# Weaving the start of each layer into the down projection of the layer before it, in a four-layer decoder trunk on eight cores

## The chip, the cores and the metric

The kernel runs on all 8 cores of one Trainium2 chip, cores 0 to 3 on one die and 4 to 7 on the other. Each core has two sequences of its own and works through them without the other cores. The time is device time of the slowest core, in microseconds (us). In slow runs the cores of a die, or of both, show a granted TensorE clock of 0.81 instead of 1.00 for part of the run, and the execution takes longer. Fast runs are compared with fast runs below, and single stages where the clock is 1.00. PE is TensorE's matmuls, PEld its weight loads, DVE VectorE, ACT ScalarE, POOL GpSimd.

## The reference

```python
# B=16, SEQ=2048 (+16 meta tokens), D_MODEL=1024, D_FF=2816, DEPTH=4, windows (2, 4, 8, 16)
for i in range(DEPTH):
    u = rms_norm(h, norm_g[i, 0])
    if i % 2 == 0: m = pool_mixer(u, ...)        # causal window means per channel group, minus u, then 256x256 matmuls
    else:          m = short_conv_mixer(u, ...)  # w_in (1024x3072), gated 3-tap conv, w_out (1024x1024)
    h = h + rms_norm(m, norm_g[i, 1])
    u = rms_norm(h, norm_g[i, 2])
    f = conv_ffn(u, ...)                         # up (1024x5632), 3-tap conv, silu(gate)*val, down (2816x1024)
    h = h + rms_norm(f, norm_g[i, 3])
```

So every sub-layer has a norm ahead of it and one behind it, and the norm ahead of a layer needs the finished h of the layer before.

## The kernel before

A core cuts its 2 x 2064 tokens into four *groups* of 1032, and a group into three *tiles* (0, 1, 2) of 344. It takes one group through all four layers, then the next. Channels lie on the partitions, so a tile of h is eight blocks of 128 x 344.

The kernel is written as a list of operations with what each reads and writes. A small list scheduler then fixes each engine's order at build time: it looks at the next few operations of an engine (the window) and takes the first whose inputs are ready by its own estimates.

```python
SCHED_WINDOW = {"pe": 12, "act": 8, "dve": 8, "pool": 10, "sp": 6}
...
finish[k] = st + o.cost + (0.25 if e == "pe" else 0.15)
```

A norm ahead of a sub-layer squares a tile whole (one ScalarE instruction), sums over the channels with eight matmuls against a matrix of ones, and gets 1/rms from Ln and Exp on ScalarE. The norm behind a sub-layer works chunk by chunk as results arrive:

```python
def norm_stats(t):
    P.op("act", I("activation", out=sq[:, :, 0:N], in_=h[:, :, o:o + N], func=AF.Square), ...)
    sbank, skey = bank("S")
    P.op("pe", [I("matmul", ps[sbank][:, 0:N], lhsT=ones[:], rhs=sq[:, c, 0:N], ...) for c in range(KC)], ...)
    return rstd_from_ss(sbank, skey, N)
...
class PostNorm:
    def chunk(self, m, pbank, pkey):     # copy to a scratch vector, square into sq[m], one ones-matmul
        ...
    def finish(self):                    # after 8 chunks: 1/rms, then per block
        # VectorE: fr = fr * g * r      GpSimd: h = h + fr
```

The down projection, called D below, is 8 chunks of 22 matmuls per tile:

```python
def ffn_d_tile(l, t):
    pn = PostNorm(l, 3, t)
    for m in range(KC):
        fb, fk = bank("C6")                        # 6 PSUM banks in turn
        P.op("pe", [... for j in range(JC)], ...)  # 22 matmuls
        pn.chunk(m, fb, fk)
    pn.finish()
```

The first projection of a convolution layer goes over four weight slots and, in each, over the tiles. With two PSUM banks per role it works in this order and no other:

```python
def sconv_s1(l):
    for sg in range(4):
        for t in range(NT):
            for mm in range(2):
                ca, va, ba = bank("A"), bank("B"), bank("C")   # shortened
                # 3 x 8 matmuls, then a few ACT and DVE steps on the PSUM results
```

A pooling layer has four stages per tile: a (norm statistics), b (window sums on VectorE), c (group matmuls and their post-norm), and the norm ahead of the feed-forward part. The main loop runs the layers one after another (cut):

```python
for li, l in enumerate(layers):
    if l % 2 == 0:
        ffn_prefetch(l)
        pool_phase(l, half)           # a, b, c, ffn_pre as a pipeline over the tiles
    else:
        for t in range(NT): sconv_pre_tile(l, t, half)
        sconv_s1(l); ffn_prefetch(l)
        for t in range(NT): sconv_s2_tile(l, t)
        for t in range(NT): ffn_pre_tile(l, t, half)
    ffn_u(l)
    ...
    for t in range(NT): ffn_d_tile(l, t)
```

## Time and profile before

The first three executions took 6521.72, 6352.34 and 6243.06 us. The profiled one was slow (6566.94 us), so stages are read where the clock is 1.00.

| Stage, core 0, clock 1.00 | us |
|---|---|
| D, three tiles | 80.4 |
| gap from D to a convolution layer's first matmul | 19.2 to 19.5 |
| its first projection, 576 matmuls | 87.9 |
| these three together ("convolution boundary") | 187.5 |
| gap from D to the up projection of a pooling layer | 86.2 to 87.6 |
| that up projection | 182.8 to 184.4 |
| D, gap and up projection ("pooling boundary") | 351 |

A group has two convolution boundaries (layers 0 to 1, 2 to 3) and one pooling boundary (1 to 2): 8 and 4 in the whole run. The rows of the stretches behind this table are shown in the prediction.

### The profile page before, as it was taken

To read this page: it belongs to the slowest core of one execution; us is meant where nothing else is said; L and a number is where in the kernel's file an instruction comes from. 1 tells how busy PE (TensorE), PEld (TensorE's weight loads), DVE (VectorE), ACT (ScalarE), POOL (GpSimd) and SP (SyncE) were. 2 spreads that over 40 slices of the span, in tenths; PEclk is the share of its full clock that TensorE was granted. 3 is DMA by queue.
4 is the path that set the end of the run, shared out by engine and by line. 5 is a ranking of instruction groups with operands and counts; after the bars stand their busy time and mean duration, and the time that the engine had idled before them with its cause. 6 is when DMAs were issued, how large, how long until landed. Compare 5 with 4: busy or idle time off the path is not lost.

```text
span 6565.4 us, 101733 instructions; the slowest of 8 cores (6455.2 to 6565.4 us)
## 1 busy us (share of the span) xinstructions
PE 5628.6 (86%) x33984; PEld 3499.4 (53%) x33984; DVE 3616.6 (55%) x6114; ACT 2391.1 (36%) x4689; POOL 1109.8 (17%) x1212
## 2 busy tenths in 40 slices
PE   3998869897798959989499886999949999789999
PEld 2655536564455636556265553655626556446555
DVE  5646474663746566464655647446356355463562
ACT  3334333433334333343433433324243233332333
POOL 2012121201212030121101212111120120211111
PEclk6999979897899979999699996877867778778777
DMA  5536243542535335353352524335144253152351
GB/s 89 70 44 84 33 65 43 72 68 71 74 46 75 52 49 69 44 84 53 74 72 43 84 32 65 43 48 76 22 94 59 33 74 52 20 74 33 52 84 30
DMA packets 433069, 385.67 MB, mean 59 GB/s; under 512 B 41072, under 2 KB 371056, under 8 KB 432560
## 3 DMA queue, kind: packets, MB, share of 16 engines
q0 software_dynamic: 422784, 345.01, 37.9%
q1 hardware_dynamic: 9776, 34.15, 1.5%
q8 instruction: 285, 4.67, 0.3%
q14 instruction: 224, 1.84, 0.1%
HBM read 707.20 MB, written 16.91 MB: 110 GB/s over the span
## 4 chain that ended last, share of the span: by engine, by line
PE 78%; DVE 10%; issue 7%; ACT 2%; DMA 2%; POOL 1%; DVEq 0%; ACTq 0%; POOLq 0%; SPq 0%
PE ps L41 78%; DVE vbuf L41 4%; DVE ugrp L41 3%; DVE actbuf L41 2%; DMA stg<-hin 1%; ACT vbuf L41 1%; POOL h L41 1%; DMA out<-stg 1%; ACT sq L41 1%; ACT stg L41 0%; DVE halom L41 0%; ACT L41 0%; DVEq L235 0%; ACTq L235 0%; ACT h L41 0%
## 5 line engine op out<-in xcount | busy, mean ns | idle before, releaser
L41 PE MATMUL ps<-ugrp,ring 128*128 128x346 bf16 (+1 forms) x21504 | 3484.4, 327 | 187.3 <-DVE ugrp L41 136.1
L41 PEld LDWEIGHTS ps<-ugrp,ring 128*128 128x128 bf16 x21504 | 2162.9, 102 | 1505.6 <-issue 306.5
L41 DVE SCALAR_TENSOR_TENSOR vbuf<-vbuf,par 128x344 f32<-128x344 f32 x1152 | 946.9, 864 | 1560.2 <-ACT vbuf L41 1542.4
L41 PE MATMUL ps<-actbuf,wa 128*128 128x344 bf16 x9984 | 1647.4, 325 | 0.0
L41 DVE SCALAR_TENSOR_TENSOR vbuf<-ps,par,vbuf 128x344 f32<-128x344 f32 x2112 | 1216.1, 576 | 255.5 <-ACT vbuf L41 147.1
L41 PEld LDWEIGHTS ps<-actbuf,wa 128*128 128x128 bf16 x9984 | 1017.7, 102 | 552.8
L41 ACT ACTIVATE vbuf<-vbuf 128x344 f32<-128x344 f32 x1248 | 610.3, 489 | 1503.3 <-DVE vbuf L41 1498.0
L41 POOL TENSOR_TENSOR h<-h,vbuf 128x344 f32<-128x344 f32 x768 | 729.0, 949 | 2160.8 <-DVE vbuf L41 1789.6
L41 DVE TENSOR_TENSOR actbuf<-vbuf,ps 128x344 bf16<-128x344 f32 x1248 | 640.3, 513 | 731.4 <-ACT vbuf L41 676.2
L41 ACT ACTIVATE vbuf<-ps 128x344 f32<-128x344 f32 (+1 forms) x768 | 351.0, 458 | 1450.5 <-PE ps L41 1443.9
L41 ACT ACTIVATE vbuf<-ps,par 128x344 f32<-128x344 f32 x1248 | 680.6, 545 | 468.1 <-PE ps L41 352.3
L41 PE MATMUL ps<-sq,ones 128*128 128x344 bf16 x1536 | 461.0, 397 | 349.4 <-ACT sq L41 347.4
L41 POOL DMA_DIRECT2D ring<-ffn_w_up x256 | 225.3, 881 | 2514.2 <-PE ps L41 2483.5
L41 PEld LDWEIGHTS ps<-sq,ones 128*128 128x128 bf16 x1536 | 177.5, 119 | 524.3 <-issue 407.0
L41 DVE SCALAR_TENSOR_TENSOR ugrp<-h,par,vbuf 128x344 bf16<-128x344 f32 x576 | 368.4, 646 | 78.5 <-ACT vbuf L41 43.4
L41 PE MATMUL ps<-ugrp,pwres 128*128 128x344 bf16 x384 | 113.7, 461 | 290.0 <-DVE ugrp L41 236.8
L41 ACT ACTIVATE sq<-h 128x2752 bf16<-128x2752 f32 x96 | 239.1, 2490 | 90.3 <-POOL h L41 90.3
L41 ACT ACTIVATE sq<-ps 128x344 bf16<-128x344 f32 x576 | 261.6, 454 | 18.5 <-PE ps L41 18.5
L41 PEld LDWEIGHTS ps<-ugrp,pwres 128*128 128x128 bf16 x384 | 51.5, 139 | 344.1 <-issue 301.3
L41 ACT ACTIVATE vbuf<-ps,epsb 128x344 f32<-128x344 f32 x192 | 104.9, 547 | 329.0 <-PE ps L41 314.7
L41 DVE SCALAR_TENSOR_TENSOR actbuf<-h,par,vbuf 128x344 f32<-128x344 f32 x192 | 114.1, 616 | 195.6 <-ACT vbuf L41 194.2
L41 DVE TENSOR_TENSOR actbuf<-actbuf 128x688 f32<-128x688 f32 (+3 forms) x240 | 211.1, 881 | 3.6
(31 smaller groups left out, 959.3 us busy)
## 6 DMA issues: line engine op xcount, KB each, us to landing
ring<-ffn_w_up POOLq DMA_DIRECT2D x224, 768.0 KB, 11.2
wa<-ffn_w_down POOLq DMA_DIRECT2D x32, 1536.0 KB, 19.1
ring<-sc_w_in POOLq DMA_DIRECT2D x96, 512.0 KB, 10.4
wa<-ffn_w_down POOLq DMA_DIRECT2D x32, 1280.0 KB, 32.9
stg<-hin SPq DMA_DIRECT2D x32, 512.0 KB, 4.5
out<-stg SPq DMA_DIRECT2D x32, 512.0 KB, 2.7
wa<-sc_w_out POOLq DMA_DIRECT2D x8, 1536.0 KB, 13.6
ring<-ffn_w_up POOLq DMA_DIRECT2D x32, 256.0 KB, 5.2
```

The costliest lines, as they stand in the source:

```text
L41: return lambda e: getattr(e, name)(*args, **kw)
```

## The change

Its intent is to fill these gaps. The operations of D for tiles 1 and 2 are written alternately, chunk by chunk, with the start of the next layer for tiles 0 and 1. The start of a convolution layer is its norm; that of a pooling layer is its norm and window sums. What belongs to tile 2 follows D. Three things go with it: a smaller scheduling window for TensorE and a latency dropped from the scheduler's estimates, weights of a pooling layer's up projection requested earlier, and fixed shares of scratch vectors and norm banks for the two interleaved streams.

```diff
+MERGE_D = True
-SCHED_WINDOW = {"pe": 12, "act": 8, "dve": 8, "pool": 10, "sp": 6}
+SCHED_WINDOW = {"pe": 8, "act": 8, "dve": 8, "pool": 10, "sp": 6}
...
+                        if e == "pe" and ops[d].eng == "pe":
+                            f -= 0.25
...
         def vec():
+            vp = ctx["vpool"]
+            if vp == "main":   # 14 of 16 scratch vectors   (cut)
+            elif vp == "bg":   # the other 2                (cut)
...
+        def merged(main_gen, bg_gen, per=1):
+            while True:
+                ctx.update(sbank=6, vpool="main")
+                ...  next(main_gen)          # one chunk of D
+                ctx.update(sbank=7, vpool="bg")
+                ...  next(bg_gen)            # one piece of the next layer's start
...
+                    if nxt is None or not MERGE_D:
+                        for t in range(NT):
+                            ffn_d_tile(l, t)
+                    else:
+                        bgf = bg_pool_gen if nxt % 2 == 0 else sconv_pre_gen
+                        ffn_d_tile(l, 0)
+                        for t in range(1, NT):
+                            merged(ffn_d_gen(l, t), bgf(nxt, t - 1, half))
+                        ctx.update(vpool="bg")
+                        gl = bgf(nxt, NT - 1, half)
+                        if nxt % 2 == 0:
+                            ctx.update(vpool=None)
+                            pool_stage_c(nxt, 0, half)
+                            ctx.update(vpool="bg")
+                        run(gl)
+                        ctx.update(vpool=None)
```

(Cut: functions turned into generators, a buffer of its own for the pooling's edge fix, the earlier `ffn_prefetch(nxt)`, and the skipping of work that has been done early.)

More of the change, by code (lines that the diff above doesn't have):

```diff
@@ L286, in build @@
         ones = sb("ones", [128, 128], BF16)
+        cfix = sb("cfix", [128, 16], F32)
         stg = [sb(f"stg{i}", [128, D], F32) for i in range(2)]
@@ L314, in region_to @@
                 reg_mode[t] = mode
-        cnts = {"psA": 0, "psB": 0, "psC": 0, "psC6": 0, "psS": 0, "vec": 0, "ring": 0, "stg": 0, "alt": 0}
+        cnts = {"psA": 0, "psB": 0, "psC": 0, "psC6": 0, "psS": 0, "vec": 0, "ring": 0, "stg": 0, "alt": 0, "vecm": 0, "vecb": 0}
         def g_ap(l, i, c):
@@ L340, in build @@
         P.op("dve", I("memset", epsb[:], EPS), writes=["eps"])
+        ctx = {"sbank": None, "vpool": None}
         def bank(role):
             if role in ("S", "T"):
+                if role == "S" and ctx["sbank"] is not None:
+                    i = ctx["sbank"]
+                    return i, f"ps{i}"
                 i = 6 + (cnts["psS"] % 2)
@@ L357, in vec @@
         def vec():
-            i = cnts["vec"] % NVEC
-            cnts["vec"] += 1
+            vp = ctx["vpool"]
+            if vp == "main":
+                i = cnts["vecm"] % (NVEC - 2)
+                cnts["vecm"] += 1
+            elif vp == "bg":
+                i = NVEC - 2 + (cnts["vecb"] % 2)
+                cnts["vecb"] += 1
+            else:
+                i = cnts["vec"] % NVEC
+                cnts["vec"] += 1
             return vecs[i], f"vec{i}"
@@ L447, in norm_stats, with prenorm_ugrp_gen @@
             return rstd_from_ss(sbank, skey, N)
-        def prenorm_ugrp(l, i, t):
+        def prenorm_ugrp_gen(l, i, t):
             o = t * N
             r, kr = norm_stats(t)
+            yield
             for c in range(KC):
@@ L455, in prenorm_ugrp, with run @@
                      reads=[hk(t), kr, "par"], writes=[f"ug{t}"], cost=0.5)
+                if c % 3 == 2:
+                    yield
+        def run(gen):
+            for _ in gen:
+                pass
+        def prenorm_ugrp(l, i, t):
+            run(prenorm_ugrp_gen(l, i, t))
         class PostNorm:
@@ L466, in chunk @@
             def chunk(self, m, pbank, pkey):
+                sq_to("chunks")
                 sc = self.scale_fn(m) if self.scale_fn is not None else 1.0
@@ L557, in ffn_pre_tile, with sconv_pre_gen, sconv_pre_tile @@
                 ugrp_halo_save(halo_f[l], f"halof{l}")
-        def sconv_pre_tile(l, t, half):
+        def sconv_pre_gen(l, t, half):
             if t == 0:
                 ugrp_halo_fill(halo_m[l], f"halom{l}", half)
-            prenorm_ugrp(l, 0, t)
+            yield from prenorm_ugrp_gen(l, 0, t)
             if t == NT - 1:
                 ugrp_halo_save(halo_m[l], f"halom{l}")
+        def sconv_pre_tile(l, t, half):
+            run(sconv_pre_gen(l, t, half))
         def ukeys_of(t):
@@ L616, in ffn_u, with ffn_d_gen @@
                     slots.append(load_wup_slot(l, sg + 2))
-        def ffn_d_tile(l, t):
+        def ffn_d_gen(l, t):
             pn = PostNorm(l, 3, t)
@@ L625, in ffn_d_tile @@
                 pn.chunk(m, fb, fk)
+                yield
             pn.finish()
+            yield
+        def ffn_d_tile(l, t):
+            run(ffn_d_gen(l, t))
+        def merged(main_gen, bg_gen, per=1):
+            alive = True
+            while True:
+                ctx.update(sbank=6, vpool="main")
+                try:
+                    next(main_gen)
+                except StopIteration:
+                    break
+                if alive:
+                    ctx.update(sbank=7, vpool="bg")
+                    for _ in range(per):
+                        try:
+                            next(bg_gen)
+                        except StopIteration:
+                            alive = False
+                            break
+            ctx.update(sbank=7, vpool="bg")
+            run(bg_gen)
+            ctx.update(sbank=None, vpool=None)
         def sconv_s1(l):
@@ L685, in pool_stage_a, with pool_stage_b_gen @@
             pool_r[t] = norm_stats(t)
-        def pool_stage_b(l, t, half):
+        def pool_stage_b_gen(l, t, half):
             o = t * N
@@ L707, in pool_stage_b @@
                      reads=[pukey], writes=[hkey], cost=0.1)
+                yield
                 cur, lo, curkey = pu, 0, pukey
@@ L719, in pool_stage_b @@
                     cur, lo, curkey = dstb, nlo, dkey_
+                yield
                 sfin = cur[:, :, HP - lo:HP - lo + N]
@@ L726, in pool_stage_b, with bg_pool_gen @@
                     for cc in range(2):
-                        tmpv, kt = vec()
-                        P.op("dve", I("tensor_tensor", out=tmpv[:, 0:16], in0=sfin[:, cc, 0:16], in1=cnt[:, g, :], op=ALU.mult),
-                             reads=[curkey, "cnt"], writes=[kt], cost=0.1)
-                        P.op("dve", I("tensor_tensor", out=ugrp[:, 2 * g + cc, HC + o:HC + o + 16], in0=tmpv[:, 0:16],
+                        P.op("dve", I("tensor_tensor", out=cfix[:, 0:16], in0=sfin[:, cc, 0:16], in1=cnt[:, g, :], op=ALU.mult),
+                             reads=[curkey, "cnt"], writes=["cfix"], cost=0.1)
+                        P.op("dve", I("tensor_tensor", out=ugrp[:, 2 * g + cc, HC + o:HC + o + 16], in0=cfix[:, 0:16],
                                       in1=pu[:, cc, HP:HP + 16], op=ALU.subtract),
-                             reads=[kt, pukey], writes=[f"ug{t}"], cost=0.1)
+                             reads=["cfix", pukey], writes=[f"ug{t}"], cost=0.1)
+        def pool_stage_b(l, t, half):
+            run(pool_stage_b_gen(l, t, half))
+        def bg_pool_gen(l, t, half):
+            pool_stage_a(l, t, half)
+            yield
+            yield from pool_stage_b_gen(l, t, half)
         def pool_stage_c(l, t, half):
@@ L745, in pool_stage_c, with pool_phase @@
             pn.finish()
-        def pool_phase(l, half):
-            stages = (pool_stage_a, pool_stage_b, pool_stage_c, ffn_pre_tile)
+        def pool_phase(l, half, skip_ab=False):
+            stages = (pool_stage_c, ffn_pre_tile) if skip_ab else (pool_stage_a, pool_stage_b, pool_stage_c, ffn_pre_tile)
             for step in range(NT + len(stages) - 1):
@@ L751, in pool_phase @@
                     t = step - k
+                    if skip_ab and st is pool_stage_c and t == 0:
+                        continue
                     if 0 <= t < NT:
@@ L807, in build @@
                 for li, l in enumerate(layers):
+                    merged_pre = MERGE_D and li > 0
                     if l % 2 == 0:
-                        ffn_prefetch(l)
-                        pool_phase(l, half)
-                    else:
-                        for t in range(NT):
-                            sconv_pre_tile(l, t, half)
+                        if l not in pre_wup:
+                            ffn_prefetch(l)
+                        pool_phase(l, half, skip_ab=merged_pre)
+                    else:
+                        if not merged_pre:
+                            for t in range(NT):
+                                sconv_pre_tile(l, t, half)
                         sconv_s1(l)
@@ L820, in build @@
                     ffn_u(l)
-                    if li + 1 < len(layers) and layers[li + 1] % 2 == 1:
-                        sconv_prefetch(layers[li + 1])
-                    for t in range(NT):
-                        ffn_d_tile(l, t)
+                    nxt = layers[li + 1] if li + 1 < len(layers) else None
+                    if nxt is not None:
+                        if nxt % 2 == 1:
+                            sconv_prefetch(nxt)
+                        else:
+                            ffn_prefetch(nxt)
+                    if nxt is None or not MERGE_D:
+                        for t in range(NT):
+                            ffn_d_tile(l, t)
+                    else:
+                        bgf = bg_pool_gen if nxt % 2 == 0 else sconv_pre_gen
[10 more added lines that the diff above has]
+                        ctx.update(vpool=None)
                 for tb in range(NBLK):
```

## The prediction

> **What bounds the kernel now.** I read four views of the profile before, in this order: spans and clocks of the cores, the page, a table of stretches of core 0 at the two kinds of layer boundary, and who waited for whom.
>
> The cores first, because the three timed runs spread from 6243 to 6522 us.
>
> ```profile
> core 0: 6565.4 us, clock 0.847
> core 4: 6455.2 us, clock 0.866
> ```
>
> The profiled run was a slow one. Cut into 100 us pieces, each core shows dense stretches at a granted clock of 1.00 for part of the run and of 0.81 for the rest (cores 0 and 1 change at about 4000 us, 4 and 5 back at about 1900 us). The unit of work repeats: four groups of tokens, each four layers. At clock 1.00 one group of core 0 lasts 1552 us (the down projection of the last layer ends at 1549.5 and at 3101.5). So a run at full clock would be 1549.5 + 3 x 1552 + 21 for the last store = 6227 us, an estimate, close to the fastest run's 6243. What is above that in the other runs is the slow clock. I therefore work at full clock and add the clock at the end.
>
> Then the page:
>
> ```profile
> PE 5628.6 (86%) x33984; PEld 3499.4 (53%) x33984; DVE 3616.6 (55%) x6114; ACT 2391.1 (36%) x4689; POOL 1109.8 (17%) x1212
> ...
> PE 78%; DVE 10%; issue 7%; ACT 2%; DMA 2%; POOL 1%; DVEq 0%; ACTq 0%; POOLq 0%; SPq 0%
> ```
>
> TensorE is the bound, but 14% of it is idle, and a tenth of the chain that ended last is VectorE. The stretches say where. Columns: length, busy time of PE, PEld, DVE, ACT, POOL, then granted clock, DMA share, GB/s.
>
> ```profile
> 313.20:393.60 80.40, 80.40 (x553) 53.81 (x550) 17.33 (x20) 22.86 (x54) 17.06 (x19) 1.00 0.27 33
> 393.60:412.90 19.30, 5.42 (x20) 2.27 (x19) 13.80 (x19) 10.96 (x11) 8.92 (x10) 0.61 0.71 109
> 417.40:501.20 83.80, 83.80 (x571) 55.44 (x570) 52.78 (x101) 24.65 (x48) 7.69 (x9) 0.99 0.45 58
> 714.40:794.80 80.40, 80.40 (x553) 53.82 (x550) 17.32 (x20) 22.88 (x54) 17.90 (x20) 1.00 0.15 19
> 794.80:882.40 87.60, 27.75 (x104) 12.74 (x102) 80.64 (x139) 38.72 (x68) 29.12 (x28) 0.61 0.18 26
> 882.40:909.60 27.20, 10.74 (x51) 5.73 (x51) 14.93 (x20) 8.64 (x10) 7.13 (x8) 0.63 1.07 163
> 909.60:1066.80 157.20, 155.66 (x1026) 97.11 (x1027) 105.94 (x200) 60.67 (x129) 13.32 (x16) 0.98 0.47 64
> ```
>
> Rows 1 and 4 are the down projection ("D") of a layer: TensorE full, VectorE 22% busy. Row 2 is the boundary before a convolution layer: 19.3 us from the last D matmul to the first of the next layer. Rows 5 and 6 are the boundary before a pooling layer: TensorE waits while VectorE is busy 80.6 of 87.6 us, and the up projection is dense only from 909.6, 114.8 us after D ended. The same gaps recur in all groups of core 0: 19.2 to 19.5 us eight times and, up to the first up-projection matmul, 86 to 88 us four times; they keep their length at clock 0.81. The waits of TensorE agree:
>
> ```profile
> PE ps L41 <- DVE ugrp L41: 372.9, 44, 15.9
> PE ps L41 <- ACT sq L41: 347.4, 152, 11.6
> ```
>
> It waits for the normalised or pooled input (written by VectorE) and for the squares of a norm (ScalarE): exactly the stages that the change moves.
>
> **What the Trainium skill says.** (1) Perfetto Trace Analysis, Optimization Strategy: where the most-contended engine changes over time, interleaving the regimes may help. That fits rows 4 and 5. (2) TensorE: Matmul & The Clock Gate, Part 2, step 1: matmuls stay in program order, only weight loads are pulled ahead. So a norm's sum matmul put into D stalls D if its squares are late; the trace shows such a stall as "<-ACT sq". (3) The same page, Part 1: dense matmuls on three cores of a die bring the clock of the whole die to 13/16. The 0.81 agrees; "the whole die" does not (cores 0 and 1 still run at 1.00 while 2 and 3 run at 0.81 before 2700 us). (4) GPSIMD Engine Reference, section 1, Specifications: GpSimd shares SBUF interfaces with VectorE and contends when a VectorE instruction has two SBUF inputs. The trace agrees with it: the scale step of a post-norm, two SBUF inputs, beside GpSimd's adds into h, has a mean of 864 ns, the one with a PSUM input 576 ns.
>
> **The change, part by part.** D of tile 0 stays. D of tiles 1 and 2 gets, between its eight chunks, the start of the next layer for tiles 0 and 1; that of tile 2 follows D. There are three such boundaries in a group: two to convolution layers, one to a pooling layer, so 8 and 4 in all. No arithmetic is added or removed; sums of the norms get a fixed PSUM bank each (6 for D, 7 for the early work) and the 16 scratch vectors are split 14 and 2.
>
> *Convolution boundary.* What is moved for one tile is a square of 2.5 us, eight ones-matmuls (1.2 us at full clock), two short activations (1.1 us) and eight VectorE steps (646 ns each, 5.2 us). D of one tile is 26.8 us (80.4 / 3) with 7.6 us of post-norm on VectorE, so this fits. The next layer starts on tile 0 at once when D ends. One weight slot on tiles 0 and 1 is 2 x 6 x 8 matmuls at 146 ns = 14.0 us. Tile 2 is ready later: evict and sum 1.5, rsqrt 1, eight post-norm steps 7.6 (one timeline entry), last add 1.2, square 2.5, ones 1.2, rsqrt 1.1, eight norm steps 5 to 7 between the layer's own VectorE work: 21 to 23 us after D. Weights for the next slot can't be used earlier, because the two PSUM banks of each role are taken in program order. So a stall of about 7 us is left, plus 2.4 us of ones-matmuls now inside D. Gain 19.3 - 7 - 2.4 = about 10 us, times 8 = 80 us.
>
> *Pooling boundary.* The pooling of one tile costs VectorE, from the groups by shape: (114.1 scale + 211.1 adds + 83.6 final + 36.1 halo copies) / 24 tiles = 18.5 us. With the post-norm 7.6 that is 26.1 us in a D of 26.8: VectorE is nearly full there, and h of a tile is final only about 12 us into the next D, its rsqrt 17 us into it. So pooling of tile 0 runs from 17 to beyond the end of D of tile 1, tile 1's starts about 21 us into D of tile 2, and some 13 of its 18.5 us are left when D ends. After D VectorE has 13 + 7.6 (post-norm of tile 2) + 7.6 (post-norm of the pooled tile 0) + 18.5 (pooling of tile 2) = 46.7 us before tile 2's group matmuls can start. Before, these start at 873.9, 79.1 us after D. That is 32 us sooner. After it come one more post-norm of tile 1 that was earlier hidden (+7), and less waiting later, since VectorE idles 9.6 us before 891.8 in the kernel before (about -10). Net about 35, less 2.4 for the ones-matmuls in D: 33 us, times 4 = 132 us.
>
> *The rest.* The scheduler's TensorE window goes from 12 to 8 and its 0.25 us latency between TensorE operations is dropped. While tile 2's pooled matmuls are not ready, 16 operations (8 + 8 ones) stand ahead of the up projection, more than either window, so this order stays: 0 us, give or take 20. The earlier weight prefetch gives nothing, since no dense stretch waits for the ring's DMA.
>
> Sum: 80 + 132 = 212 us. Full clock: 6227 - 212 = 6015 us, ratio 0.966.
>
> **The rivals.**
> - *D stalls.* There is one buffer of squares, used whole by an early norm and in chunks by D's own sums. From chunk 1 on, D's squares wait until the early norm's eight ones-matmuls are done, some 17 to 20 us into D. D survives because six PSUM banks hold its chunks (6 x 3.35 = 20 us). If the squares are 5 us later (VectorE busy with pooling), each merged D stalls by that: 5 x 8 tiles before pooling layers and less in the 16 before convolution layers, 40 to 80 us back. For it: row 5's VectorE load. Against: banks and my times just fit. Time then about 6080.
> - *VectorE becomes the bound of the pooling boundary.* It is in my sum; if GpSimd's adds stretch pooling from 18.5 to 22 us, everything runs over by another 4 us per tile: 10 us x 4 = 40 us back.
> - *The clock takes it back.* Denser TensorE work could keep more cores at 0.81. A wholly slow group costs about 220 us more (the last one takes 6541.2 - 4769.4 = 1772 us from D's end to D's end, against 1552). For: 0.81 is seen only in dense phases. Against: the cores change state in the long gaps, and full-clock runs have dense phases of 280 us. Then 6150 to 6300 in a slow run, with nothing wrong in the schedule.
> - *A better tail.* Were the up projection let in before tile 2's pooled matmuls, 15 us more per pooling boundary: 5950.
>
> **Range and chances.** Runs before have a median 125 us above full clock. After, I take 6015 + about 105 = 6120 us. The low end, 5980, is full clock with a slightly better tail; the high end, 6290, is a run as slow as the middle ones before plus a stalling D. Faster by over 2% needs 125 us of the 212; both boundaries would have to give half of what I expect for it to fail. Faster 0.82, within 2% 0.15, slower 0.03.
>
> **What would show it.** Right: the boundary before convolution layers shrinks from 19.3 us to near zero with a stall of 5 to 9 us some 14 us later; the table of stretches shows VectorE over 80% busy in D of tiles 1 and 2 before a pooling layer; the gap from D to the first up-projection matmul is 50 to 60 us instead of 87; a three-tile D stays within 80.4 + 3 us at clock 1.00. Wrong: D longer than 86 us, with waits for squares inside it (rival 1); a pooling gap over 70 us (rival 2); same gaps gained but the dense stretches at 0.81 for longer (rival 3).

## The result, and the profile after

On the same chip, 13 executions of each:

| | fast runs, us | median of all | range of all |
|---|---|---|---|
| before | 6240.64 to 6249.09 (seven), 6291.63 | 6249.09 | 6240.64 to 7018.77 |
| after | 6117.10 to 6120.38 (six) | 6236.01 | 6117.10 to 6877.29 |

The ratio of fast runs is 0.9791, with a 95% interval of 0.9766 to 0.9815. Ratios here are the mean time of one kernel's fast runs over that of the other's in the same rounds, so they are not quite the ratio of the medians that are quoted. The change is faster, by about 2%. Whether by more than 2% is unclear: the interval lies on both sides of that line, and without the one run of 6291.63 us, which counts as fast, the ratio of means is 6118.6 / 6243.3 = 0.980. In fast runs it gained about 123 us, where 212 had been worked out for full clock.

The profiled execution after was a slow one. First its clocks by die, then lines of the page for all engines and for the chain that ended last, then three of TensorE's waits on core 0 (total us, count, mean):

```profile
die 0 (median of its cores): 6206.5 us, clock 0.899
die 1 (median of its cores): 6224.5 us, clock 0.897
```

```profile
PE 5390.3 (86%) x33984; PEld 3387.8 (54%) x33984; DVE 3604.8 (58%) x6114; ACT 2375.5 (38%) x4689; POOL 1113.2 (18%) x1212
...
PE 76%; DVE 10%; issue 7%; ACT 3%; POOL 2%; DMA 2%; DVEq 0%; ACTq 0%; POOLq 0%; SPq 0%
```

```profile
PE ps L42 <- ACT sq L42: 295.3, 146, 11.6
...
PE ps L42 <- DVE ugrp L42: 259.7, 33, 16.5
...
PE ps L42 <- DVE vbuf L42: 78.3, 32, 6.2
```

The counts of instructions are the same as before. TensorE's share of the span is still 86%: busy time and span shrank together, because less of this run was at 0.81, so this share says nothing about the change. The waits do: those for the normalised or pooled input (`ugrp`) fell from 372.9 to 259.7 us and those for squares from 347.4 to 295.3. But the wait for `vbuf` has doubled, from 37.4 us in 16 waits to 78.3 in 32. Here TensorE waits for VectorE to read a PSUM bank (a product into a scratch vector) before it may overwrite it.

**The convolution boundary.** Stretches of core 0 before: the gap, then the first 10.8 us of the projection. Columns as in the prediction.

```profile
2698.30:2717.70 19.40, 5.39 (x19) 2.26 (x19) 13.92 (x19) 10.96 (x11) 8.99 (x10) 0.59 0.69 108
2717.70:2728.50 10.80, 10.80 (x59) 6.55 (x60) 7.78 (x16) 2.20 (x5) 0.00 (x0) 0.79 0.01 2
```

The same boundary after: D, the projection's first matmuls, a hole, and the rest in two parts.

```profile
2665.70:2747.90 82.20, 82.20 (x564) 54.88 (x563) 27.08 (x37) 29.68 (x60) 16.93 (x19) 1.00 0.25 31
2748.50:2758.20 9.70, 9.68 (x67) 6.20 (x64) 6.84 (x8) 2.75 (x6) 6.62 (x8) 1.00 0.71 111
2758.20:2769.00 10.80, 2.41 (x9) 1.11 (x10) 2.51 (x5) 4.00 (x4) 2.09 (x3) 0.75 0.50 94
2769.00:2785.20 16.20, 16.20 (x95) 9.85 (x96) 13.43 (x29) 4.31 (x8) 2.67 (x3) 0.85 0.13 16
2785.20:2846.30 61.10, 61.10 (x420) 40.50 (x418) 37.07 (x69) 17.76 (x34) 4.75 (x6) 1.00 0.54 74
```

The gap behind D is 0.6 us now (2747.9 to 2748.5), and then TensorE works for 9.7 us and is nearly idle for 10.8: 2.41 us busy, with 9 matmuls. The projection takes 97.9 to 102.4 us (100.4 on average) instead of 87.9, and D takes 82.2 instead of 80.4. Together 183.3 instead of 187.5: of the 19.3 us, 4.2 are gained. The timeline of TensorE, VectorE and ScalarE says what the hole is (start, length; in brackets the engine's idle time ahead and who ended it):

```profile
2749.81 8.37 PE L42 MATMUL ps<-ugrp,ring 128*128 128x346 bf16 x56
...
2751.36 7.57 DVE L42 SCALAR_TENSOR_TENSOR vbuf<-vbuf,par 128x344 f32<-128x344 f32 x8 [3.18 <-ACT vbuf L42]
...
2760.79 2.50 ACT L42 ACTIVATE sq<-h 128x2752 bf16<-128x2752 f32 x1 [1.62 <-POOL h L42]
...
2763.43 2.36 PE L42 MATMUL ps<-sq,ones 128*128 128x344 bf16 x8 [5.25 <-ACT sq L42]
...
2767.12 1.26 DVE L42 SCALAR_TENSOR_TENSOR ugrp<-h,par,vbuf 128x344 bf16<-128x344 f32 x2 [8.19 <-ACT vbuf L42]
...
2768.30 0.51 DVE L42 TENSOR_TENSOR vbuf<-vbuf,ps 128x346 f32<-128x346 f32 x1
...
2768.95 16.28 PE L42 MATMUL ps<-ugrp,ring 128*128 128x346 bf16 x94 [3.16 <-DVE vbuf L42]
```

This is tile 2's chain, link by link: its post-norm on VectorE, the adds on GpSimd, the square, the ones-matmuls, 1/rms, the norm steps. Its first link filled the gap before as well: there VectorE did tile 2's post-norm (7.57 us, as now) ahead of tile 0's norm, for which the first matmul waited. The first 64 matmuls, on tiles 0 and 1, cover 9.4 us of the chain (the 56 shown take 8.37). Then two more things hold TensorE. It reaches the ones-matmuls of tile 2 in its fixed order and waits 5.25 us for the square. And the projection's first VectorE step (2768.30, product of a PSUM result and a scratch vector) stands in VectorE's order behind tile 2's first two norm steps, so that the two banks of the role come free only then: 3.16 us more, "<-DVE vbuf".

**The pooling boundary**, core 0 after: D of tiles 0, 1 and 2, the time up to tile 2's group matmuls, from there to the dense up projection, and that.

```profile
2330.80:2357.50 26.70, 26.70 (x185) 17.92 (x184) 2.10 (x4) 7.00 (x17) 1.45 (x2) 1.00 0.65 90
2357.50:2386.00 28.50, 28.50 (x197) 19.01 (x196) 14.29 (x22) 12.78 (x24) 7.25 (x8) 1.00 0.01 1
2386.00:2414.20 28.20, 27.06 (x186) 17.98 (x185) 22.39 (x35) 9.77 (x19) 8.01 (x8) 1.00 0.00 1
2414.20:2474.60 60.40, 18.56 (x71) 7.41 (x68) 52.51 (x74) 25.01 (x46) 23.28 (x22) 0.59 0.00 1
2474.60:2510.00 35.40, 16.71 (x72) 8.71 (x73) 23.49 (x33) 15.83 (x27) 13.03 (x15) 0.64 0.91 141
2510.00:2665.80 155.80, 154.98 (x1026) 96.52 (x1027) 104.69 (x198) 60.76 (x129) 13.38 (x16) 0.99 0.46 65
```

VectorE was busy 17.3 us in the 80.4 us of D before; now it is 2.10 + 14.29 + 22.39 = 38.8 us. That is the moved work. But in the fourth row it still has 52.51 us to do, in 60.40, and TensorE's 18.56 us lie beside it. The gap from D to the first up-projection matmul is 64.7 us on average over three such boundaries (62.0 to 68.9) instead of 87, D is 85.2 instead of 80.4, and the total is 332.8 (328.6 to 335.0) instead of 351: a gain of 18 us (over all cores, in the boundaries without the clock of 0.81: 351.0 and 333.0). The fifth row is as long as before: there it was 35.7 us (873.9 to 909.6), here it is 35.4.

Three waits inside these rows, from the timeline of the same core:

```profile
2410.74 0.31 PE L42 MATMUL ps<-sq,ones 128*128 128x344 bf16 x1 [1.14 <-ACT sq L42]
...
2430.82 0.99 ACT L42 ACTIVATE vbuf<-ps,par 128x344 f32<-128x344 f32 x2 [11.01 <-DVE vbuf L42]
...
2491.28 7.57 DVE L42 SCALAR_TENSOR_TENSOR vbuf<-vbuf,par 128x344 f32<-128x344 f32 x8 [8.28 <-ACT vbuf L42]
```

The first is D itself waiting for squares. In the second the eviction of tile 0's group matmuls waits 11 us for a scratch vector that VectorE has yet to read, and VectorE is then idle for 6.67 us. That makes this boundary an exception: from D's end to tile 2's group matmuls it takes 60.4 us, and 50.5 to 52.5 at the other three of this core, where VectorE is busy 97% of the time. The third is in the fifth row: VectorE, the bound of the row above, is idle for 8.28 us, because here it waits on the chain of one tile.

### The profile page after: what moved, and what is told of

It reads as the page before. It is cut to its first block, busy times and chain, and to the rows that moved or that the text cites. A ratio compares the mean times of both kernels' runs of the same rounds, so it can differ in the third digit from the quotient of the medians.

```text
span 6234.5 us, 101591 instructions; the slowest of 8 cores (6191.8 to 6234.5 us)
## 1 busy us (share of the span) xinstructions
PE 5390.3 (86%) x33984; PEld 3387.8 (54%) x33984; DVE 3604.8 (58%) x6114; ACT 2375.5 (38%) x4689; POOL 1113.2 (18%) x1212
## 4 chain that ended last, share of the span: by engine, by line
PE 76%; DVE 10%; issue 7%; ACT 3%; POOL 2%; DMA 2%; DVEq 0%; ACTq 0%; POOLq 0%; SPq 0%
PE ps L42 76%; DVE vbuf L42 4%; DVE ugrp L42 3%; DVE actbuf L42 2%; POOL h L42 2%; ACT vbuf L42 2%; DMA stg<-hin 1%; ACT sq L42 1%; DMA out<-stg 1%; ACT stg L42 0%; DVE halom L42 0%; DVEq L238 0%; ACT L42 0%; ACTq L238 0%; POOLq L238 0%
## 5 line engine op out<-in xcount | busy, mean ns | idle before, releaser
L42 PE MATMUL ps<-ugrp,ring 128*128 128x346 bf16 (+1 forms) x21504 | 3352.4, 318 | 190.5 <-DVE ugrp L42 84.1
L42 PEld LDWEIGHTS ps<-ugrp,ring 128*128 128x128 bf16 x21504 | 2093.0, 99 | 1447.0 <-issue 352.3
L42 PE MATMUL ps<-actbuf,wa 128*128 128x344 bf16 x9984 | 1555.8, 314 | 0.0
L42 PEld LDWEIGHTS ps<-actbuf,wa 128*128 128x128 bf16 x9984 | 990.9, 99 | 504.6
L42 PE MATMUL ps<-sq,ones 128*128 128x344 bf16 x1536 | 411.7, 373 | 293.4 <-ACT sq L42 290.9
L42 ACT ACTIVATE sq<-h 128x2752 bf16<-128x2752 f32 x96 | 239.2, 2492 | 101.9 <-POOL h L42 101.9
```

The source lines that it names most:

```text
L42: return lambda e: getattr(e, name)(*args, **kw)
```

## The experiments

Twelve kernels ran. Each diff is against the kernel after unless it says otherwise. "Undisturbed die" is a die that stayed at full clock in an execution whose other die did not.

**1 to 3: which part gives what.** The merge for convolution layers alone, for pooling layers alone, and for none (all the rest of the change kept). In these rounds no run of the kernel before was at full clock (the lowest, 6342.16 us, had all cores at 0.89 to 0.90), so there are no ratios.

```diff
# convolution only
-merged_pre = MERGE_D and li > 0
+merged_pre = MERGE_D and li > 0 and l % 2 == 1
-if nxt is None or not MERGE_D:
+if nxt is None or not MERGE_D or nxt % 2 == 0:
# pooling only: the same with the parities swapped
# nothing merged:
-MERGE_D = True
+MERGE_D = False
```

> Only the 8 boundaries before convolution layers are merged into the down projection; those before pooling layers run as in the kernel before. From the two traces (187.5 us from start of the down projection to the end of the first convolution projection before, 183.3 after) the theory expects 4.2 us x 8 = 34 us under the kernel before, so about 6209 us in a fast run; up to 19 us less if the scheduler's new window and latency give the unexplained rest. My prediction's size (10 us each) would give 6163.

> Only the 4 boundaries before pooling layers are merged. From the traces (351 us from start of the down projection to the end of the up projection before, 333 after): 17 to 18 us x 4 = 70 us under the kernel before, about 6173 us in a fast run, up to 19 us less with the scheduler's part. My prediction's size (33 us each) would give 6111.

> Nothing is merged; only the scheduler's TensorE window of 8, the dropped latency between TensorE operations and the earlier weight prefetch stay. If these give the 19 us that the boundaries do not explain, a fast run is about 6224 us; if they give nothing, as predicted, 6243.

With nothing merged the one fast run took 6220.49 us, with the boundaries about as before (187.9 and, over all cores, 349.8 us). So 23 us of the gain come from the small parts of the change; run 11 says more about where. With pooling alone the lowest run took 6145.85, 75 us less than that (a second one, 6176.44, counts as fast although one die ran some 25 us behind the other). The pooling boundaries are 328.4 to 333.9 us there, the convolution boundaries as before. With convolution alone all six runs were slow (lowest 6307.15), so I read the undisturbed die of that run: its cores took 6186.7 to 6196.4 us (the same die with nothing merged: 6210.9 to 6218.6), about 25 us less, with convolution boundaries of 183 us. As far as lowest runs and one die can say, the parts add up: 6243 - 23 - 25 - 75 = 6120, where the whole change takes 6117 to 6120. Against the 80 and 132 us of the prediction, both merges gave less, and the "0, give or take 20" gave 23.

**4: is it VectorE's order that leaves the hole?** In the timeline the projection's first VectorE step stands behind tile 2's norm. If the scheduler's window for VectorE is wider, it can take that step earlier.

```diff
-SCHED_WINDOW = {"pe": 8, "act": 8, "dve": 8, "pool": 10, "sp": 6}
+SCHED_WINDOW = {"pe": 8, "act": 8, "dve": 16, "pool": 10, "sp": 6}
```

> The changed kernel with the scheduler's VectorE window at 16 instead of 8. Theory: the eight waiting norm steps of tile 2 fill the window of 8 and put the convolution layer's first VectorE steps behind them in the fixed order, so PSUM banks are not freed and TensorE stops after 8 of 12 matmul groups. Then the stall falls from about 11 us to 5 to 7 and a fast run is 6117 - 8 x 4 = about 6085 us, with VectorE's first convolution step within 5 us of the first matmuls. Rival: tile 2's late norm alone sets the stall; then the time stays at 6117 (+-6).

The fast run took 6121.03 us: nothing gained. The timeline of core 0, where D ended at about 2649.7:

```profile
2660.67 0.93 DVE L42 TENSOR_TENSOR vbuf<-vbuf,ps 128x346 f32<-128x346 f32 x2
...
2664.69 1.33 PE L42 MATMUL ps<-ugrp,ring 128*128 128x344 bf16 x8 [0.87 <-DVE actbuf L42]
...
2669.32 5.34 DVE L42 SCALAR_TENSOR_TENSOR ugrp<-h,par,vbuf 128x344 bf16<-128x344 f32 x8 [0.29 <-ACT vbuf L42]
...
2674.81 10.38 PE L42 MATMUL ps<-ugrp,ring 128*128 128x346 bf16 x53 [6.82 <-DVE ugrp L42]
```

The steps did come forward: the product now runs 11 us after D's end instead of 20. TensorE finished the first slot on tiles 0 and 1, and then waited 6.82 us for tile 2's norm, whose last step ends at 2674.66, 25 us after D, as it did without this edit. The projection is 99.95 us long (99.8 over all cores, 100.4 in the kernel after). My theory that the window alone hid the gain fell; behind that limit stood a second one, tile 2's chain.

**5 and 6: what sets the pooling gap, and what stalls D?** The first gives tile 0's group matmuls scratch vectors out of the 14 of the main stream, so that their eviction does not wait as seen above. The second gives the early norms a squares buffer of their own (laid over the staging buffers), so that D's squares need not wait for it.

```diff
# 5
-                            ctx.update(vpool=None)
+                            ctx.update(vpool="main")
                             pool_stage_c(nxt, 0, half)
# 6 (cut: the same buffer in the instructions that follow)
+            if ctx["vpool"] == "bg":
+                sqb, sqk = sqn, ["stg0", "stg1"]
+            else:
+                sq_to("whole")
+                sqb, sqk = sq, ["sq"]
```

> The changed kernel, but the group matmuls of pooled tile 0 (the stage issued right after the merged down projection) take their scratch vectors in turn from the 14 of the main pool, where five are free, instead of from the common count of 16, where the copies waited 11 us for vectors that tile 2's post-norm still held. Theory (a wait for scratch vectors delays pooled tile 0's post-norm, VectorE then idles 6.7 us and all after it is late): the gap from the down projection to the up projection before pooling layers falls from 62-69 us to 55-60, a fast run is 6117 - 4 x 6 = about 6093 us. Rival (VectorE's total work sets the gap whatever the order): 6117 (+-6).

> The changed kernel, but the early norms of the next layer write their squares to a buffer of their own (the idle staging buffers). Rival 1 of the prediction (the shared buffer of squares stalls the down projection): its length before pooling layers falls from 83.4-88.7 us to 82.2 and before convolution layers stays at 82.2, a fast run is 6117 - 4 x 3 = about 6105 us. If the shared squares also held the chain of tile 2 or the tail, more than 20 us less.

Run 5 had fast runs of 6118.13 and 6115.32 us, ratio 0.9798 (0.9769 to 0.9826): no change against the kernel after, where 6093 had been the theory's time, so the rival stands. The rows up to tile 2's group matmuls, and from there to the up projection, on core 0:

```profile
2314.80:2367.80 53.00, 17.53 (x71) 7.81 (x69) 52.06 (x74) 25.20 (x46) 23.60 (x22) 0.59 0.00 1
2367.80:2402.00 34.20, 17.20 (x72) 8.74 (x72) 21.39 (x29) 15.78 (x26) 13.18 (x15) 0.65 0.96 143
```

With the wait gone, VectorE is busy 52.06 of 53.00 us: there is nothing left in this row but its work. The boundary takes 329.6 us on average, some 3 us less, which is too little to stand out in the time. Only one boundary in four, the one shown above, had lost time to it.

Run 6 shortened D before pooling layers only to 82.7 to 86.7 us, and its fast runs took 6129.89 and 6132.91 us (a third, 6180.98, counts as fast although one die ran some 50 us behind the other); ratio 0.9848 (0.9774 to 0.9921). I had expected 6105, so this was a miss. Over all cores D before a pooling layer is shorter by 1.4 us (84.2 instead of 85.6), so the shared buffer is part of the stall, but the whole is slower by 12. The traces say where: a convolution boundary takes 184.6 us instead of 183.2, and eight of them make 11 us. Why its projection is longer (101.9 us instead of 100.4) was not found.

**7 and 12: more cover for tile 2's chain.** If the projection works on the second slot of weights for tiles 0 and 1 before it turns to tile 2, there are 28 us of matmuls to cover the chain instead of 14. Run 7 has this order and the wider VectorE window of run 4; run 12 has the order alone.

```diff
-            for sg in range(4):
+            for sg, t in ((0, 0), (0, 1), (1, 0), (1, 1), (0, 2), (1, 2),
+                          (2, 0), (2, 1), (2, 2), (3, 0), (3, 1), (3, 2)):
...
-                if sg + 2 < 4:
+                if t == NT - 1 and sg + 2 < 4:
```

> As e4 (VectorE window 16), but the first convolution projection does tiles 0 and 1 of two weight slots (28 us of matmuls at full clock) before tile 2, instead of one slot (14 us). Theory (before convolution layers the end is set by tile 2's own chain, ready about 25 us after the down projection, and only 14 us of matmuls cover it): the projection's length falls from about 100 us to 86-92 (weights of slots 2 and 3 may come up to 4 us late), a fast run is 6117 - 8 x 10 = about 6037 us. Rival (VectorE's load or the PSUM banks set it): less than 3 us per boundary, above 6093.

> e7's order of the convolution projection with the VectorE window back at 8. Theory (two limits one behind the other: with a window of 8 the eight waiting norm steps of tile 2 hold back the projection's own VectorE steps, so TensorE stops after 8 groups whatever work is in line behind; only with both removed does the stall shrink): no gain over the changed kernel, projection about 100 us long, a fast run 6117 (+-8). If the order alone is what e7 gained from: about 6090, 94 us long.

Run 7 had fast runs of 6084.68, 6087.17 and 6099.76 us, ratio 0.9756 (0.9734 to 0.9778), so some 32 us faster than the kernel after (lowest against lowest), and faster than the kernel before by over 2%. On core 4 the projection took 88.0 to 99.1 us, 94.3 on average (95.5 over all cores, where the clock is 1.00). One boundary of core 4 with 88 us, and then one with 95:

```profile
3430.68 13.06 PE L42 MATMUL ps<-ugrp,ring 128*128 128x346 bf16 x88
...
3459.69 57.90 PE L42 MATMUL ps<-ugrp,ring 128*128 128x346 bf16 x392 [1.50 <-DVE ugrp L42]
```

```profile
2672.00 20.78 PE L42 MATMUL ps<-ugrp,ring 128*128 128x344 bf16 x128 [5.44 <-DVE actbuf L42]
...
2693.32 42.40 PE L42 MATMUL ps<-ugrp,ring 128*128 128x346 bf16 x288 [0.55 <-DMA ring<-sc_w_in]
```

In the first the wait for tile 2's norm is down to 1.50 us. In the second TensorE waits 5.44 us for a step that frees a bank of another role (its result goes to `actbuf`). I had expected 6037, a gain of 80 us: the direction was right and the size less than half. The boundary gave 4.9 us (178.3 instead of 183.2 over all cores), eight times 39 us; but with the wider window, in runs 4 and 7 alike, the up projection of the pooling layers is some 2 us longer (185.1 to 185.5 us on average, 182.6 to 183.0 in the kernel after).

Run 12 took 6114.11 us, with projections of 100.4 us on average over all cores. The order alone gives nothing, the window alone gave nothing (run 4), both give 32 us. At the boundary itself it is the same: 183.2 us in the kernel after, 182.6 with the window, 183.2 with the order, 178.3 with both. Two limits stood one behind the other here: with VectorE's order fixed too early, more matmuls can't be issued because the banks don't come free; with the order right, there are too few matmuls.

**8 and 9: how far it goes.** Run 8 has edits 5, 6 (which alone was slower) and 7, and an up projection in the same order (two slots on tiles 0 and 1 ahead of tile 2). Run 9 adds to it the interleaving of the norm ahead of the feed-forward part with the second projection (s2) of a convolution layer, and early squares of their own in nearly all norms.

```diff
# 8, besides 5, 6, 7
-            for sg in range(nsg):
+            for sg, t in [(0, 0), (1, 0), (0, 1), (1, 1), (0, 2), (1, 2)] + [(g_, t_) for g_ in range(2, nsg) for t_ in range(NT)]:
# 9, against 8 (cut: the squares)
-                        for t in range(NT):
-                            sconv_s2_tile(l, t)
-                        for t in range(NT):
-                            ffn_pre_tile(l, t, half)
+                        sconv_s2_tile(l, 0)
+                        for t in range(1, NT):
+                            sconv_s2_tile(l, t)
+                            ffn_pre_tile(l, t - 1, half)
+                        ffn_pre_tile(l, NT - 1, half)
```

> e5, e6 and e7 together, and the same order in the up projection: two weight slots of tile 0, then of tile 1, then of tile 2. If the effects add: about 6117 - 24 - 12 - 80 = 6000 us, and the up projection's stall of 28 us in pooling layers (182-184 us long against 154.5 of matmuls) falls by about 7 us, in all layers by up to 10 us x 16: 5850 to 5970 us. If its weights come too late for the new order, no gain in the up projection: about 6000.

> e8, and the same two means at the boundary that the change left alone: the feed-forward norms of tiles 0 and 1 are issued between the output projections of tiles 1 and 2 of a convolution layer, with squares of their own, so that the up projection starts at once and covers tile 2's chain of about 26 us with 28 us of matmuls. Theory: the gap of 19.6 us after the output projection (8 times) closes and at most 5 us of stall come back: e8's 6068 - 8 x 12 to 18 = 5925 to 5975 us in a fast run. If the chain can't be covered so (VectorE's order or weights): above 6030.

Run 8: 6066.65 to 6071.10 us, ratio 0.9721 (0.9693 to 0.9749). Run 9: 6057.31 to 6059.28, ratio 0.9703 (0.9675 to 0.9731), the best of all and better than both kernels. Both fell well short of what I expected (5850 to 5970 or 6000, and 5925 to 5975). In run 9 the gap behind s2 went from 19.7 to 10.8 us, and yet the stretch from the start of s2 to the end of the up projection did not shrink (217.3 us over all cores, 216.1 in run 8, 214.1 in the kernel after). The time came back inside the up projection (core 7):

```profile
1250.89 6.13 PE L42 MATMUL ps<-ugrp,ring 128*128 128x346 bf16 x32 [6.64 <-DVE ugrp L42]
...
1262.68 5.96 PE L42 MATMUL ps<-ugrp,ring 128*128 128x346 bf16 x24 [4.49 <-DVE vbuf L42]
```

A tile of s2 is about 10 us, which by these waits is too short to cover a tile's norm; the expectation of run 9 had named this case (above 6030). The 10 us by which run 9 still beats run 8 lie elsewhere: the up projection of the pooling layers takes 179.0 us over all cores, 181.3 to 182.4 in run 8. Which part of edit 9 does that was not separated.

**10: is the pooling gap VectorE's work?** Layer 2 gets only the first of its window adds, 4 instead of 10 per tile. Its output is wrong, which doesn't matter for the time.

```diff
-                for s_ in range(g + 1):
+                for s_ in range(1 if l == 2 else g + 1):
```

> The changed kernel with one window add per group instead of 1, 2, 3 and 4 in layer 2, the only merged pooling layer (its output is wrong on purpose; the later layers' work is the same). It takes 6 adds of 0.8 us pitch, 4.8 us, of VectorE work from each tile. Rival 2 of the prediction (VectorE's total work sets the gap before pooled tile 2): the part of tile 1's pooling that is left after the down projection and all of tile 2's shrink, so the gap to the up projection falls from 62-69 us by about 8 to 10 us, and a fast run by 4 x 9 = 36 us to about 6081 us; the tail from tile 2's group matmuls to the dense up projection stays at 35 us. If waits and not work set the gap: less than 3 us per boundary, 6105 or more.

The fast run took 6083.77 us, where 6081 was expected; the undisturbed dies of the others took 6071 to 6079. D, the row up to tile 2's group matmuls, and the row behind it, on core 3:

```profile
2218.70:2300.90 82.20, 82.20 (x565) 54.92 (x563) 35.61 (x57) 29.56 (x60) 16.42 (x18) 1.00 0.24 32
2300.90:2344.80 43.90, 18.33 (x72) 7.76 (x70) 35.25 (x54) 24.18 (x45) 16.16 (x17) 0.63 0.00 1
2344.80:2386.40 41.60, 17.78 (x72) 8.94 (x73) 28.81 (x38) 16.20 (x28) 17.44 (x20) 0.62 0.79 119
```

The row before tile 2's group matmuls fell from 50 to 60 us to 43.9 (54.0 to 41.8 on average over all cores), and VectorE's work in it from about 51 to 35.25. So VectorE's work sets it in the kernel after. The adds also stand on tile 2's own chain, but they make only about 5 us there, and the row fell by more than twice that. With the adds gone VectorE is no longer full here (35.25 of 43.90 us). D is 82.2 us in three of the four boundaries, without the stalls: D stalls where VectorE is late with the post-norm and pooling; the shared squares buffer is only part of it (run 6). The row behind was to stay at 35 us and is 41.6: part of the work moved into it. The whole boundary took 322 us instead of 333.

**11: do the 23 us come from the window?** Nothing merged, and TensorE's window back at 12.

```diff
-MERGE_D = True
+MERGE_D = False
-SCHED_WINDOW = {"pe": 8, "act": 8, "dve": 8, "pool": 10, "sp": 6}
+SCHED_WINDOW = {"pe": 12, "act": 8, "dve": 8, "pool": 10, "sp": 6}
```

> e3 (nothing merged) with TensorE's scheduler window back at 12; of the change only the dropped 0.25 us between TensorE operations and the place of the weight prefetch are left. If the window of 8 gave e3's 23 us: a fast run is 6243 us; if the latency or the prefetch gave them: 6220. No theory of mine prefers one; I expect the window, since it changes which matmul goes first where several are ready (60 to 40).

Fast runs of 6220.57 and 6226.82 us, beside 6220.49 with the window at 8: no difference beyond the spread, and I had bet 60 to 40 on the window. (The kernel before took 6239.52 to 6241.00 us in the same rounds, so the rest of the change gives 19 us by this measure.) What is left is the dropped latency of 0.25 us, the place of the prefetch or the new buffer for the edge fix; no run separates them. The traces of runs 3 and 11 do say where the time went. The up projection of the pooling layers takes 182.1 us on average instead of 183.9, eight times, which is about 14 us; and the gap behind s2 is 0.6 us shorter, eight times.

## Why the prediction was right or wrong

*The result as a whole.* The time on record was 6120 us. The median of 13 runs is 6236, inside the range and 116 us above 6120; the fast runs at 6117 to 6120 look like a hit, but it is partly a coincidence. The sum said 6015 us for a run at full clock, and 105 us were added for the slow clock that most runs have. At full clock the change gave about 123 us instead of 212. "Faster by over 2%", with a chance of 0.82, fell on that line: 2.1%, with an interval from 1.9 to 2.3%.

*What bounds the kernel: right.* The gaps were the two kinds of boundary, and merging acts on them: runs 1 to 3 put 25 us on the convolution boundaries and 75 us on the pooling ones.

*Convolution boundary, 10 us each: 4.2 measured.* The form was right (no gap behind D, then a stall), and so was the ones-matmuls' cost (2.4 expected, D grew by 1.8 to 2.1). The term that failed is "a stall of about 7 us is left". It was 12.5 on average (100.4 - 87.9; 9.9 at the boundary shown). Most of the miss is that tile 2 was ready 25.7 us after D (2747.9 to 2773.6), not 21 to 23 (and the 7 us took the low end, 21 - 14). VectorE began its post-norm 3.5 us after D (2.5 expected), the square came 1.9 us behind the post-norm (1.2 expected), and the ones-matmuls took 2.36 us and not 1.2: from 2763.4 to 2765.9, after 5 us without a matmul, the granted clock was 0.53. Even with all of the cover of 14.0 us this leaves 11 to 12 us. Before the hole only 9.4 of the cover was used, as the projection's first VectorE steps stood behind tile 2's, and the rest ran late. This second limit cost little by itself: run 4 used the whole cover, and the projection stayed at 99.95 us. The low clock behind the hole is no third reason. Over the first 10.8 us of matmuls it is 0.78 (2769.0 to 2779.8), and it was 0.79 in the kernel before, so that the 87.9 us contain it. The prediction assumed that the matmuls of a slot run on; it checked TensorE's order and the PSUM banks, and not the order of VectorE, which frees these banks. Runs 4, 7 and 12 show that both the order and the cover limit it.

*Pooling boundary, 33 us each: 18 measured.* The mechanism was right: VectorE full, TensorE waiting for tile 2. Three terms were off.
- "46.7 us" of VectorE work after D was 49.2 to 52.5, and tile 2's group matmuls started 54.0 us after D on average over all cores: 25 us sooner than before, not 32. The prediction counted tile 1's post-norm, 7.6 us, as coming after them (the "+7"); in the timeline of the boundary shown, six of its eight steps came ahead of them.
- "Less waiting later (about -10)" did not happen: at that boundary the stretch from tile 2's group matmuls to the dense up projection was 35.7 us before and 35.4 after. There VectorE waits for one tile's chain (8.28 us idle), and having less to do does not shorten that.
- "2.4" for ones-matmuls in D was 4.8 on average and up to 8.3, with the stalls.

*The rest, 0 us give or take 20: 19 to 23 measured.* Run 3 has it and run 11 clears the window; most of it lies in the up projection of the pooling layers. I had argued that the order of TensorE would stay where tile 2's matmuls wait, and looked nowhere else.

*The rivals.* Rival 1, stalls of D, is real and small: 4.8 - 2.4 us at four boundaries, about 10 us, and nothing at the convolution ones. The rival named a shared buffer and late squares. With less VectorE work nearly all of the stall goes (run 10, 82.5 us on average); with a squares buffer of its own part of it goes (run 6, 84.2 instead of 85.6), at a loss elsewhere. Rival 2, VectorE as the bound of the pooling gap, holds: runs 5 and 10. Rival 3, the clock, is not seen: 7 of 13 runs after and 5 of 13 before are slow, too few to tell apart, and in the fast runs 3 and 5 all eight cores hold 1.00 in the dense stretches that I read. Rival 4, a better tail, did not come by itself. With the up projection reordered as well (run 8) the up projection of the merged pooling layer took 181.3 us on average over all cores, 183.0 in the kernel after and 185.2 in run 7, which has the same wide window.

## What to carry to other kernels

Starting the next stage early pays only as far as the last tile's own chain is covered by matmuls on the other tiles: measure that chain from end to end at the gap's own pace and count the cover, before merging. Check that the engine which frees the buffers of the covering work has it in its order in time; of two limits one behind the other, removing either alone shows nothing, so try both together before giving up on one. Where a second engine is full at a boundary, moving its work gives only what it can do in the idle time elsewhere, and the part behind it that waits for one tile's chain stays as long as it was.

## What the Trainium skill lacked or had wrong

- "TensorE: Matmul & The Clock Gate", Part 1, says that three busy cores take the whole die to 13/16 and that 1.95 GHz is to be budgeted for sustained dense matmuls on all cores. In the profile before, cores 0 and 1 were still at 1.00 while 2 and 3 were at 0.81. In two profiled fast runs (6220.49 us with nothing merged, 6118.13 us in run 5) all eight cores hold 1.00 through dense stretches of 50 to 110 us at the same time. What tips an execution into the slow state stays open.
- "GPSIMD Engine Reference", section 1, says that VectorE instructions with two SBUF inputs contend with GpSimd and gives no size there (other pages of the skill say more on this contention). On core 0 after, the same norm step (two SBUF inputs, bf16 result) has a mean of 575 ns in 505 places where no GpSimd add into h ran beside it, and of about 1017 ns in 36 places where one ran during most of it. Eight such steps took 5.34 us without adds; eight of a post-norm took 7.57 us beside eight adds. (The 864 ns of the prediction are the mean of a group of 1152, of which 384 are steps of the convolution.)
- No page that I read says how to size such interleaving: that the last tile's chain, here 25.7 us, must be covered by other work, here at most 14.0 us, or the gap comes back as a stall. Of 19.3 us of gap 4.2 were gained.
